# Hybrid SSD and RG-LRU block: 28 column tiles of the input projection computed in pairs of seven half-block products

## Chip, cores and metric

One core of a Trainium2 chip. The metric is the device time of one execution in microseconds (us); the kernel before takes 2112.51 us, the median of three runs (2111.7 to 2112.93).

## What is computed

One decoder block on 1024 tokens and 1024 channels, in float32:

```
hn = RMSNorm(h)
[gates | z | xBC | dt | lru_x | lru_gate] = hn @ W_in
y_ssm = W_o_ssm( GatedRMSNorm( SSD(conv(xBC)) + D*x , silu(z) ) )
y_lru = W_o_lru( RG-LRU(conv(lru_x)) * gelu(lru_gate) )
h = h + W_out( sigmoid(g_ssm) * y_ssm + sigmoid(g_lru) * y_lru )
h = h + SwiGLU(RMSNorm(h))
```

with a final RMSNorm. W_in has 16 column tiles of 128 for the gates, 10 for lru_x (LX), 10 for lru_gate (LG), and those of z, x, B and C of the SSD. The RG-LRU is, for each of 10 columns of 128 channels, a causal conv of width 4, two 128x128 gate products with sigmoids, and a scan over the tokens; its result is multiplied by gelu of the LG column.

## The kernel before

The layout is channels on partitions and tokens along the row. Every float32 operand is split into a high and a low part in TensorE's fp32r format (`split`: ACT casts the high part, L98; DVE subtracts to get the low part, L99), and every product is three matmuls, high by high, low by high and high by low (`mm3`, L168 to 177). A projection column tile is 2 token halves x 8 channel blocks x 3 = 48 matmuls of 128x512. The instructions of an engine run in the order that a scheduler gave them; each waits for semaphores of the others. All transfers are issued in order by one queue, SP.

The stages, in order: the first four gate tiles with the norm; the SSD, 64 steps (4 groups, 2 halves, 8 chunks) between whose small products 46 projection tiles are spread as fill (`fills`); the RG-LRU stage (about 760 to 1045 us), ten times LX tile, LG tile, `lru_gates` (L785 on), then two gate tiles; w_out_ssm, w_out_lru and w_out; the FFN's input product (about 1413 to 1855), and its output product.

In the RG-LRU stage `lx_done` runs the conv (ACT L491, three DVE steps L494) and splits u; `lg_done` is the gelu (L782). `lru_gates` does 12 matmuls, four tanh or exp steps on ACT, three DVE steps (L810, L808, L811), the scan (L812) and the multiply by the gelu (L813), all on DVE. POOL has nothing there. The first eight operands of w_out_ssm (`y0`) are loaded and split in this stage.

The FFN's input product is already done in pairs. For two column tiles with weights of two 512-channel halves, and two token halves, seven products of half blocks (512 channels by 512 tokens, 4 x 3 = 12 matmuls each) take the place of eight. They need sums of weights, made by POOL for each pair (`pair_sums`, L924 to L927, into buffers of their own), sums of the operands (t1 to t4), made once in w_out's second half, and combinations of the results, made by DVE from PSUM (L1030 to L1052).

Of the kernel before, what the change touches and what calls it, by code (L numbers as in the profile page):

```python
# [67 lines left out]
def hybrid_block(ctx, tc, xT, w_in, w_dt, w_os, w_ol, w_o, w_fi, w_fo, w_fl, lru_w, params, heads, out):  # L68
# [219 lines left out]
    with ExitStack() as st1:  # L288
        cst = st1.enter_context(tc.tile_pool(name="cst", bufs=1, reuse_waits="tile", side="right"))
        dt = cst.tile([P, NCH, NH], F32, name="dt")  # L290
# [468 lines left out]
        tp = ctx.enter_context(tc.tile_pool(name="tp", bufs=NTMP, reuse_waits="tile"))  # L759
        ar0 = ctx.enter_context(tc.tile_pool(name="ar0", bufs=8, reuse_waits="tile"))  # L760


        with tc.tile_pool(name="lru", bufs=1, reuse_waits="tile", side="right") as lp, tc.tile_pool(
            name="lps", bufs=2, space=PSUM
        ) as lps:
            u_, gl_ = {}, {}

            def lx_done(j):
                def done(ps):
                    u = lp.tile([P, T], F32, name="u", bufs=2)  # L770
                    conv(u, ps, [pcol("lcw", j * 4 + i) for i in range(4)], pcol("lcb", j))
                    uh = lp.tile([P, T], F32R, name="uh")
                    ul = lp.tile([P, T], F32R, name="ul")
                    split(uh, ul, u)
                    u_[j] = u, uh, ul

                return done

            def lg_done(j):
                def done(ps):  # L780
                    gl = lp.tile([P, T], F32, name="gl")
                    S.activation(gl, ps, AF.Gelu_apprx_tanh)  # L782
                    gl_[j] = gl

                return done  # L785

            def lru_gates(j):
                u, uh, ul = u_.pop(j)
                raw = lp.tile([P, 2, P], F32, name="lraw", bufs=2)
                load(raw, lru_w[:, j])  # L790
                gw = lp.tile([P, 2, P], F32R, name="lwh", bufs=2)
                gl = lp.tile([P, 2, P], F32R, name="lwl", bufs=2)
                split(gw, gl, raw)
                th = []
                for q, bname in ((0, hbr), (1, hbi)):
                    gp = lps.tile([P, T], F32, name="gp", tag="gp")
                    for c in hcol:
                        mm3(gp[:, c], lambda k: (gw[:, q, :], gl[:, q, :]), [(uh[:, c], ul[:, c])])
                    t_ = lp.tile([P, T], F32, name=f"lth{q}", bufs=2 - q)
                    S.activation(t_, gp, AF.Tanh, bias=bname[:, j : j + 1], scale=0.5)  # L800
                    th.append(t_)
                a = lp.tile([P, T], F32, name="a", bufs=2)
                S.activation(a, th[0], AF.Exp, bias=cc[:, j : j + 1], scale=cc[:, j : j + 1])

                S.activation(th[0], th[0], AF.Tanh, bias=ncc[:, j : j + 1], scale=ncc[:, j : j + 1])
                a2 = lp.tile([P, T], F32, name="a2")
                S.activation(a2, a, AF.Square)
                V.scalar_tensor_tensor(th[0], a2, 1.0, th[0], op0=ALU.add, op1=ALU.mult)  # L808
                S.activation(th[0], th[0], AF.Sqrt)
                V.scalar_tensor_tensor(u, th[1], 1.0, u, op0=ALU.add, op1=ALU.mult)  # L810
                V.scalar_tensor_tensor(u, u, 0.5, th[0], op0=ALU.mult, op1=ALU.mult)  # L811
                V.tensor_tensor_scan(a, a, u, 0.0, op0=ALU.mult, op1=ALU.add)  # L812
                V.tensor_tensor(a, a, gl_.pop(j), op=ALU.mult)  # L813
                store(yl_d[j], a)

            for j in range(NLRU):
                project_now(lx_done(j))
                project_now(lg_done(j))
                lru_gates(j)

            def gate_done(i):
                def done(ps):
                    gt = lp.tile([P, T], F32, name="gl")
                    S.activation(gt, ps, AF.Tanh, bias=hgb[:, i : i + 1], scale=0.5)
                    store(gate_d[i], gt)

                return done


            y0 = [act_pair(ar0, load_half(yn_d[i][:, hcol[0]])) for i in range(8)]  # L830
            for i in range(16 - last_gates, 16):
                project_now(gate_done(i))
# [58 lines left out]
    for d in range(KD):
        mg[1][d] = act_pair(ar1, res[d][:, 1, :])

    raws, wops = {}, {}

    def pair_load(j):
        raws[j] = []
        for q in range(2):
            raw = wpool.tile([P, KD, P], F32, name="raw", tag="raw", bufs=2)
            load(raw, w_fi[q * NFF + j])
            raws[j].append(raw)

    def pair_a1(j):  # L910
        raw = raws[j][0]
        hi = wpool.tile([P, KD, P], F32R, name="whi", tag="whi")
        lo = wpool.tile([P, KD, P], F32R, name="wlo", tag="wlo")
        split(hi, lo, raw)
        wops[j] = {"a11": (hi[:, 0:4, :], lo[:, 0:4, :]), "a12": (hi[:, 4:8, :], lo[:, 4:8, :])}
# [322 lines left out]
```

## Time and profile before

| what | value |
| --- | --- |
| median of three runs | 2112.51 us |
| the profiled execution | 2113.38 us |
| its span, first to last instruction | 2111.4 us |
| mean granted TensorE clock | 0.989 |
| TensorE, DVE, ACT, POOL busy | 98%, 60%, 41%, 19% |
| RG-LRU stage, 800 to 1000 us: TensorE, DVE, ACT | 100%, 59%, 65% |

A busy share is an average over stages; how a stage stands is read from the table of busy times by stretch, and what TensorE waited for from its list of waits. A matmul's recorded duration (about 390 ns) is longer than its distance to the next one, since matmuls are pipelined; the distance comes from how many start in a stretch.

### The profile page before, as it was taken

What the parts mean: (1) busy time and instruction counts of PE and PEld (TensorE: products, weight loads), DVE (VectorE), ACT (ScalarE), POOL (GpSimd) and SP (SyncE); (2) the same over time, 40 slices, a digit from 0 to 9 for tenths busy, and PEclk for the clock granted to TensorE, in tenths of its full rate; (3) what the DMA queues carried; (4) which work ended last, traced back from release to release, by engine and by line L of the source; (5) the groups of instructions that cost most, each with busy time, mean ns of one, the idle gap of its engine ahead of it and who ended that gap; (6) DMA issues with size and microseconds to landing.
All of it is one profiled execution on the core that took longest, in us unless ns stands there. A gap on an engine that the chain in (4) does not pass through costs nothing.

```text
span 2111.4 us, 24842 instructions
## 1 busy us (share of the span) xinstructions
PE 2066.4 (98%) x9702; PEld 1681.2 (80%) x9702; DVE 1261.3 (60%) x1587; ACT 856.0 (41%) x1253; POOL 406.7 (19%) x378
## 2 busy tenths in 40 slices
PE   8999999999999999999999999988999999999998
PEld 6677887887887888888888888866888888878887
DVE  8655567567667546555514544588666666654336
ACT  5334445445455436666513221453223222233124
POOL 5103333334343410000000000234322332100000
PEclk8999999999999999999999999999999999999999
DMA  3222223323223243211314431542222222283122
GB/s 140 88 62 88 85 77 117 103 75 113 88 77 118 89 159 135 75 65 60 128 52 159 144 114 58 162 148 97 67 87 90 82 70 88 74 287 107 52 59 80
DMA packets 99973, 212.17 MB, mean 100 GB/s; under 512 B 11024, under 2 KB 29456, under 8 KB 99856
## 3 DMA queue, kind: packets, MB, share of 16 engines
q1 hardware_dynamic: 99856, 210.59, 30.9%
q8 instruction: 76, 1.25, 0.2%
q14 instruction: 41, 0.34, 0.1%
HBM read 168.34 MB, written 42.21 MB: 100 GB/s over the span
## 4 chain that ended last, share of the span: by engine, by line
PE 87%; DVE 5%; issue 2%; POOL 2%; ACT 2%; DMA 1%; SPq 0%; DVEq 0%; POOLq 0%; ACTq 0%
PE pj L175 12%; PE pj L177 11%; PE pj L176 11%; PE pbk L175 9%; PE pbk L177 9%; PE pbk L176 9%; PE pbk L960 6%; PE pbk L962 6%; PE pbk L961 6%; PE yb L661 1%; PE yb L649 1%; DVE xs L494 1%; PE tr L627 1%; DVE wlo L99 1%; DVE xl L332 1%
## 5 line engine op out<-in xcount | busy, mean ns | idle before, releaser
L175 PE MATMUL pj<-hnh,whi 128*128 128x512 f32 x1152 | 461.0, 400 | 0.0
L177 PE MATMUL pj<-hnl,whi 128*128 128x512 f32 x1152 | 452.8, 393 | 0.0
L176 PE MATMUL pj<-hnh,wlo 128*128 128x512 f32 x1152 | 451.7, 392 | 0.0
L177 PE MATMUL pbk<-un,whi 128*128 128x512 f32 x816 | 317.8, 390 | 1.3 <-DVE un L99 1.3
L175 PE MATMUL pbk<-un,whi 128*128 128x512 f32 x816 | 317.9, 390 | 1.0 <-ACT un L98 1.0
L176 PE MATMUL pbk<-un,wlo 128*128 128x512 f32 x816 | 317.3, 389 | 0.0
L98 ACT CAST whi<-raw 128x1024 fp32r<-128x1024 f32 (+3 forms) x172 | 167.2, 972 | 308.8 <-PE pbk L177 199.7
L99 DVE TENSOR_TENSOR wlo<-raw,whi 128x1024 fp32r<-128x1024 f32 (+3 forms) x172 | 201.5, 1172 | 142.8 <-ACT whi L98 140.9
L177 PEld LDWEIGHTS pj<-hnl,whi 128*128 128x128 f32 x1152 | 216.6, 188 | 48.1 <-issue 0.5
L175 PEld LDWEIGHTS pj<-hnh,whi 128*128 128x128 f32 x1152 | 216.7, 188 | 45.8 <-issue 2.4
L176 PEld LDWEIGHTS pj<-hnh,wlo 128*128 128x128 f32 x1152 | 216.9, 188 | 44.9 <-issue 1.4
L177 PEld LDWEIGHTS pbk<-un,whi 128*128 128x128 f32 x816 | 153.2, 188 | 35.2 <-DVE un L99 3.2
L175 PEld LDWEIGHTS pbk<-un,whi 128*128 128x128 f32 x816 | 153.2, 188 | 33.3 <-ACT un L98 1.7
L176 PEld LDWEIGHTS pbk<-un,wlo 128*128 128x128 f32 x816 | 153.2, 188 | 31.8 <-issue 0.2
L960 PE MATMUL pbk<-xh,sh 128*128 128x512 f32 x352 | 140.1, 399 | 13.2 <-ACT sh L98 10.0
L857 POOL TENSOR_TENSOR rs<-rs,sq 128x512 f32<-128x512 f32 x14 | 22.7, 1620 | 639.2 <-ACT sq L856 639.2
L961 PE MATMUL pbk<-xh,sl 128*128 128x512 f32 x352 | 137.3, 390 | 0.4 <-DVE sl L99 0.4
L962 PE MATMUL pbk<-xl,sh 128*128 128x512 f32 x352 | 137.3, 390 | 0.0
L620 ACT ACTIVATE E<-csb,cs 128x128 f32<-128x128 f32 x256 | 82.8, 392 | 107.6 <-PE yb L661 100.4
L98 ACT CAST sh<-s 128x1024 fp32r<-128x1024 f32 x44 | 46.3, 1052 | 171.3 <-PE pbk L961 157.8
L960 PEld LDWEIGHTS pbk<-xh,sh 128*128 128x128 f32 x352 | 66.1, 188 | 35.1 <-ACT sh L98 10.4
L1089 DVE TENSOR_TENSOR res<-res,pbk 128x512 f32<-128x512 f32 x48 | 32.8, 686 | 87.4 <-PE pbk L177 87.4
(265 smaller groups left out, 3366.3 us busy)
## 6 DMA issues: line engine op xcount, KB each, us to landing
raw<-in_w_in SPq DMA_DIRECT2D x74, 512.0 KB, 3.5
raw<-in_w_fi SPq DMA_DIRECT2D x44, 512.0 KB, 3.9
csb<-cs_d SPq DMA_DIRECT2D x64, 256.0 KB, 3.5
ld<-act_d SPq DMA_DIRECT2D x44, 256.0 KB, 5.4
yn_d<-xs SPq DMA_DIRECT2D x16, 512.0 KB, 3.2
ld<-yn_d SPq DMA_DIRECT2D x32, 256.0 KB, 5.2
raw<-in_w_os SPq DMA_DIRECT2D x16, 512.0 KB, 3.5
gt<-gate_d SPq DMA_DIRECT2D x32, 256.0 KB, 4.1
```

Source lines behind the costliest of these rows:

```text
L98: S.copy(hi, src)
L99: V.tensor_tensor(lo, src, hi.bitcast(F32), op=ALU.subtract)
L175: PE.matmul(ps, wh, xh, start=i == 0, stop=False)
L176: PE.matmul(ps, wl, xh, start=False, stop=False)
L177: PE.matmul(ps, wh, xl, start=False, stop=i == n - 1)
L332: V.scalar_tensor_tensor(lo, x, pcol("n1", k), hi.bitcast(F32), op0=ALU.mult, op1=ALU.subtract)
L620: S.activation(E[:, j, :], csb[:, j, :], AF.Relu, bias=cs[:, c, h0 + j : h0 + j + 1], scale=-1.0)
L857: G.tensor_tensor(acc, acc, sq, op=ALU.add)
L960: PE.matmul(ps, wh, xh, start=first and k == 0, stop=False, skip_group_check=True)
L961: PE.matmul(ps, wl, xh, start=False, stop=False, skip_group_check=True)
L962: PE.matmul(ps, wh, xl, start=False, stop=last and k == 3, skip_group_check=True)
L1089: V.tensor_tensor(r, r, ps, op=ALU.add)
```

## The change

Gates 6 to 15 and LX and LG 1 to 9, 28 tiles, are taken out of the SSD's fill and the RG-LRU stage and computed as 14 pairs of seven products, in the order LX1/LG1, LX2/LG2, gates 6/7, LX3/LG3, and so on. LX0 and LG0 are still computed directly, and only gates 4 and 5 stay in the SSD's fill (38 fill tiles). In detail:

- hn is stored to memory as it is made (16 stores), reloaded behind the SSD, and made into t1 to t4 by `t_parts` (four subtractions or additions L837 to L840 and two splits for each of four channel blocks).
- `pair_sums` (L809 to L812) leaves three of its four sums in the raw weight buffers themselves; these are freed only when the last split of the pair (`pair_s`) has read them.
- The RG-LRU of a column is a generator, `lru`, with a piece run between the products of the next pair (`pump`). Its last multiply goes from DVE to POOL.
- Combinations: `c11` (ACT copies or the gate's tanh), then DVE L870, L874, L875, L879 and L883; the FFN uses the same `pair`.
- The operands of w_out_ssm are no longer loaded ahead. w_out's second half goes through columns 4 to 7 first, then 0 to 3, with `t_parts` on the latter. FFN results are stored per column instead of per half.
- Pools: room of hn's second half, blocks 0 to 3 (`hnq`), is taken over by the buffers of the pair stage (`ar` with 30 units and `sp1`).

```diff
-            fills[g, 0] = x_tiles(g, 1) + z_tiles(g, 0) + [PJ_GATE + gate_next + i for i in range(n)]
+        fills[g, 0] = x_tiles(g, 1) + z_tiles(g, 0)
...
+                    store(hn_d[k][:, hcol[h]], xr[h][k])
...
+    def pair_sums(n):
+        g_, u_ = raws[n]
+        s1 = sp1.tile([P, H], F32, name="ws1", tag="ws1")
+        wops[n]["raw1"] = s1
+        G.tensor_tensor(blk(s1), u_[:, 0:4, :], u_[:, 4:8, :], op=ALU.add)
+        G.tensor_tensor(u_[:, 0:4, :], u_[:, 0:4, :], g_[:, 0:4, :], op=ALU.add)
+        G.tensor_tensor(g_[:, 0:4, :], g_[:, 0:4, :], blk(s1), op=ALU.add)
+        G.tensor_tensor(g_[:, 4:8, :], g_[:, 4:8, :], g_[:, 0:4, :], op=ALU.add)
...
+    def pair(n, x, c11, pump, nxt=None, first=False, cpool=None):
+        wo = wops.pop(n)
...
+        px, pv = bank(), bank()
+        product(px, wo["a11"], x["b11"], True, False)
+        S.copy(c1[:, 0, :], px)
+        pump()
...
+            product(pv, wo["s1"], x["t1"], True, False)
+            pump()
+            product(px, wo["a12"], x["b21"], False, True)
+        prep(pair_a1)
+        prep(pair_sums)
+        py = bank()
+        product(py, wo["s2"], x["t2"], True, False)
+        c11(c0, px)
+        V.tensor_tensor(c0[:, 1, :], c1[:, 0, :], py, op=ALU.subtract)
+        pump()
+        product(py, wo["s3"], x["t3"], False, True)
+        prep(pair_s1)
+        V.tensor_tensor(c1[:, 0, :], py, c1[:, 0, :], op=ALU.subtract)
+        V.tensor_tensor(c1[:, 1, :], c1[:, 0, :], pv, op=ALU.subtract)
+        pump()
+        pz = bank()
+        product(pz, wo["a22"], x["t4"], True, True)
+        V.tensor_tensor(c1[:, 0, :], pz, c1[:, 0, :], op=ALU.add)
+        prep(pair_s, 1)
+        pump()
+        product(pv, wo["s4"], x["b22"], False, True)
+        V.tensor_tensor(c0[:, 1, :], c0[:, 1, :], pv, op=ALU.add)
+        prep(pair_s, 0)
+        pump()
+        return c0, c1
...
+    for k in range(4):
+        t_parts(x1, k, bs.pop(k), bs.pop(k + 4))
...
+    for n, (f0, f1) in enumerate(ppairs):
+        nxt = n + 1 if n + 1 < len(ppairs) else None
+        if nxt:
+            pair_load(nxt, [w_in[f] for f in ppairs[nxt]])
+        if f0 >= PJ_LX:
+            c0, c1 = pair(n, x1, copy_c11, pump, nxt)
+            sides.append(lru(f0 - PJ_LX, c1, c0))
...
-    res = [unit(ar1, F32, "res") for d in range(KD)]
+    yn = [load_acts(yn_d[:8], h) for h in range(2)]
```

How the order moves on DVE, at three places. First the entry into the RG-LRU stage. Before, behind the SSD's last reciprocals: splits of weights (wlo, lwl), the last scaling of the SSD's results (xs) and the conv of LX0 (u, L494):

```order
L99 TENSOR_TENSOR wlo<-raw,whi 128x1024
L713 SCALAR_TENSOR_TENSOR xs<-xs,par,acc 128x1024 x4
L99 TENSOR_TENSOR wlo<-raw,whi 128x1024
L99 TENSOR_TENSOR lwl<-lraw,lwh 128x256
L494 SCALAR_TENSOR_TENSOR u<-pj,par,u 128x1023
L99 TENSOR_TENSOR wlo<-raw,whi 128x1024
L494 SCALAR_TENSOR_TENSOR u<-pj,par,u 128x1022
L99 TENSOR_TENSOR lwl<-lraw,lwh 128x256
L494 SCALAR_TENSOR_TENSOR u<-pj,par,u 128x1021
```

And with the change; b is reloaded hn, xth and xtl are the split t operands:

```order
L838 TENSOR_TENSOR b<-b 128x512
L99 TENSOR_TENSOR lw<-lraw,lw 128x256
L839 TENSOR_TENSOR b<-b 128x512
L840 TENSOR_TENSOR b<-b 128x512
L99 TENSOR_TENSOR xtl<-b,xth 128x1024
L837 TENSOR_TENSOR b<-b 128x512
L99 TENSOR_TENSOR xtl<-b,xth 128x1024
L838 TENSOR_TENSOR b<-b 128x512
L839 TENSOR_TENSOR b<-b 128x512
L840 TENSOR_TENSOR b<-b 128x512
L505 SCALAR_TENSOR_TENSOR u<-pj,par,u 128x1023
L99 TENSOR_TENSOR xtl<-b,xth 128x1024
```

The conv of LX0 now stands behind three groups of t operands; its other two steps follow with the third group's last split between them.

Second, inside the stage with the change, pair 2 (gates 6 and 7) with the RG-LRU of columns 1 and 2 beside it; pbk is a PSUM bank, c_ the two result tiles of a pair, the rows on a, u and lth are the RG-LRU's:

```order
L924 SCALAR_TENSOR_TENSOR u<-u,lth_6646 128x1024
L870 TENSOR_TENSOR c_6713<-c_6714,pbk 128x512
L925 SCALAR_TENSOR_TENSOR a<-a,u 128x1024
L505 SCALAR_TENSOR_TENSOR u<-c_6544,par,u 128x1023
L99 TENSOR_TENSOR lw<-lraw,lw 128x256
L505 SCALAR_TENSOR_TENSOR u<-c_6544,par,u 128x1022
L874 TENSOR_TENSOR c_6714<-pbk,c_6714 128x512
L505 SCALAR_TENSOR_TENSOR u<-c_6544,par,u 128x1021
L875 TENSOR_TENSOR c_6714<-c_6714,pbk 128x512
L879 TENSOR_TENSOR c_6714<-pbk,c_6714 128x512
L99 TENSOR_TENSOR ul<-u,uh 128x1024
L99 TENSOR_TENSOR wsl<-raw,wsh 128x1024
```

Between the first and the second reading of a product's bank (L870, L874) stand the scan and two conv steps.

Third, the exit. Before, in the end of the RG-LRU stage; un are the split operands of w_out_ssm's second half of tokens, those of the first half were made earlier:

```order
L811 SCALAR_TENSOR_TENSOR u<-u,lth_8163 128x1024
L99 TENSOR_TENSOR wlo<-raw,whi 128x1024
L812 SCALAR_TENSOR_TENSOR a<-a,u 128x1024
L813 TENSOR_TENSOR a<-a,gl 128x1024
L99 TENSOR_TENSOR wlo<-raw,whi 128x1024
L99 TENSOR_TENSOR un<-ld,un 128x512 x8
L99 TENSOR_TENSOR wlo<-raw,whi 128x1024 x7
```

With the change:

```order
L879 TENSOR_TENSOR c_8417<-pbk,c_8417 128x512
L919 SCALAR_TENSOR_TENSOR u<-lth_8512,u 128x1024
L921 SCALAR_TENSOR_TENSOR lth_8487<-a_8538,lth_8487 128x1024
L883 TENSOR_TENSOR c_8416<-c_8416,pbk 128x512
L924 SCALAR_TENSOR_TENSOR u<-u,lth_8487 128x1024
L925 SCALAR_TENSOR_TENSOR a<-a,u 128x1024
L99 TENSOR_TENSOR un<-ld,un 128x512 x16
L99 TENSOR_TENSOR wlo<-raw,whi 128x1024 x7
```

All 16 splits of w_out_ssm's first operands stand behind the last scan.

## Rows read from the trace of the kernel before

**Rows 1.** The page, busy time, share of the span and count by engine.

```profile
PE 2066.4 (98%) x9702; PEld 1681.2 (80%) x9702; DVE 1261.3 (60%) x1587; ACT 856.0 (41%) x1253; POOL 406.7 (19%) x378
```

**Rows 2.** Table by stretch: PE, PEld, DVE, ACT, POOL busy (count), clock, DMA share, GB/s.

```profile
760.00:800.00 40.00, 40.00 (x174) 32.49 (x173) 25.52 (x24) 20.61 (x26) 0.00 (x0) 1.00 0.66 231
800.00:900.00 100.00, 100.00 (x438) 81.91 (x437) 59.30 (x49) 65.73 (x62) 0.00 (x0) 1.00 0.25 84
...
1400.00:1500.00 100.00, 85.24 (x362) 67.67 (x361) 81.58 (x84) 40.48 (x56) 41.75 (x28) 0.95 0.29 96
1500.00:1600.00 100.00, 100.00 (x438) 81.20 (x437) 67.01 (x78) 28.20 (x36) 29.49 (x21) 1.00 0.26 80
...
1440.00:1850.00 410.00, 406.77 (x1776) 330.62 (x1776) 273.47 (x317) 116.41 (x150) 117.50 (x82) 1.00 0.27 84
160.00:750.00 590.00, 586.41 (x3120) 473.71 (x3117) 384.07 (x540) 281.82 (x503) 205.41 (x233) 1.00 0.30 93
```

**Rows 3.** TensorE's waits: waiting line, releaser, us in all, times, longest.

```profile
PE pbk L960 <- ACT sh L98: 10.0, 1, 10.0
...
PE st L177 <- POOL xddl L638: 3.2, 8, 1.1
```

**Rows 4.** Table by stretch around the start of the FFN.

```profile
1420.00:1424.00 4.00, 0.00 (x0) 0.00 (x0) 3.87 (x5) 0.70 (x2) 1.52 (x1) 0.65 0.00 0
1424.00:1428.00 4.00, 0.00 (x0) 0.00 (x0) 3.43 (x3) 2.14 (x4) 3.93 (x3) 0.50 0.17 66
1428.00:1432.00 4.00, 3.43 (x6) 1.63 (x7) 4.00 (x4) 3.81 (x7) 2.36 (x2) 0.57 0.16 32
1432.00:1436.00 4.00, 4.00 (x20) 3.24 (x19) 4.00 (x6) 1.64 (x2) 0.00 (x0) 1.00 0.49 168
```

**Rows 5.** Groups of DVE instructions in the RG-LRU stage: busy us, mean ns | idle before.

```profile
L99 DVE TENSOR_TENSOR wlo<-raw,whi 128x1024 fp32r<-128x1024 f32 x21 | 25.6, 1221 | 23.9 <-ACT whi L98 23.9
L812 DVE TENSOR_TENSOR_SCAN a<-a,u 128x1024 f32<-128x1024 f32 x10 | 22.8, 2281 | 0.0
L494 DVE SCALAR_TENSOR_TENSOR u<-pj,par,u 128x1023 f32<-128x1023 f32 x10 | 12.8, 1280 | 13.8 <-ACT u L491 13.8
...
L810 DVE SCALAR_TENSOR_TENSOR u<-lth,u 128x1024 f32<-128x1024 f32 x10 | 12.2, 1225 | 38.5 <-ACT lth L800 38.5
...
L99 DVE TENSOR_TENSOR un<-ld,un 128x512 fp32r<-128x512 f32 x8 | 5.0, 684 | 0.0
L99 DVE TENSOR_TENSOR lwl<-lraw,lwh 128x256 fp32r<-128x256 f32 x10 | 4.2, 420 | 8.4 <-ACT lwh L98 8.4
```

**Rows 6.** Groups of DVE instructions in the FFN pairs, 1440 to 1850.

```profile
L1044 DVE TENSOR_TENSOR sg<-sg,s 128x512 f32<-128x512 f32 x21 | 34.0, 1618 | 0.7
...
L1043 DVE TENSOR_TENSOR s<-s,rs 128x512 f32<-128x512 f32 x21 | 22.7, 1082 | 0.7
...
L1033 DVE TENSOR_TENSOR u<-s,pbk 128x512 f32<-128x512 f32 x22 | 15.1, 688 | 9.1 <-PE pbk L962 9.1
```

**Rows 7.** Groups of POOL instructions in the FFN pairs, 1440 to 1850.

```profile
L927 POOL TENSOR_TENSOR s<-s,raw 128x512 f32<-128x512 f32 x21 | 35.9, 1711 | 0.2
L926 POOL TENSOR_TENSOR s<-raw 128x512 f32<-128x512 f32 x20 | 29.1, 1456 | 15.0 <-PE pbk L962 15.0
L925 POOL TENSOR_TENSOR s<-s,raw 128x512 f32<-128x512 f32 x21 | 27.6, 1317 | 1.5
L924 POOL TENSOR_TENSOR s<-raw 128x512 f32<-128x512 f32 x20 | 25.8, 1288 | 243.1 <-DVE sl L99 236.2 <-DVE su L1038 6.9
```

**Rows 8.** The page's DMA issues, KB each, us from issue to landing.

```profile
raw<-in_w_in SPq DMA_DIRECT2D x74, 512.0 KB, 3.5
```

**Rows 9.** Groups of ACT instructions in the RG-LRU stage, 780 to 1045.

```profile
L98 ACT CAST whi<-raw 128x1024 fp32r<-128x1024 f32 x22 | 22.8, 1036 | 1.9 <-PE pj L177 1.9
...
L782 ACT ACT_TABLE_LOAD x10 | 12.8, 1283 | 0.2
...
L782 ACT ACTIVATE gl<-pj 128x1024 f32<-128x1024 f32 x10 | 10.3, 1028 | 2.6 <-PE pj L177 2.6
```

More of the change, by code (lines that the diff above doesn't have):

```diff
@@ L61 @@
 NTMP = 13
-NUNIT = 29
+NUNIT = 30
 FFG = ((0, 6), (6, 12), (12, 17), (17, 22))
@@ L757, in hybrid_block @@
                 pass
[L759 to L832, printed above, removed]
@@ new lines, in hybrid_block, with hn_load, lx0_done @@
+    x1 = {
+        "b11": [hn[0][k] for k in range(4)],
+        "b21": [hn[0][4 + k] for k in range(4)],
+        "b22": [hn[1][4 + k] for k in range(4)],
+        **{t: [None] * 4 for t in ("t1", "t2", "t3", "t4")},
+    }
+    bs = {}
+    def hn_load(k):
+        for i in (k, k + 4):
+            bs[i] = unit(ar, F32, "b")
+            load(row(bs[i]), hn_d[i])
+    u0, gl0 = unit(ar, F32, "u"), unit(ar, F32, "c1")
+    def lx0_done(ps):
+        conv(row(u0), ps, [pcol("lcw", i) for i in range(4)], pcol("lcb", 0))
@@ new lines, in lg0_done @@
+    def lg0_done(ps):
+        S.activation(row(gl0), ps, AF.Gelu_apprx_tanh)
+    hn_load(0)
+    hn_load(1)
+    pieces = [project(lx0_done), project(lg0_done)]
+    for k in range(4):
+        t_parts(x1, k, bs.pop(k), bs.pop(k + 4))
+        if k < 2:
+            hn_load(k + 2)
+        if k == 3:
+            pair_load(0, [w_in[f] for f in ppairs[0]])
+        for _ in range(2):
+            next(pieces[k // 2], None)
+    for q in pieces:
+        for _ in q:
+            pass
+    pair_a1(0)
@@ L848, in mm_act, with load_acts @@
+    while sides:
+        pump()
+    st_hn.close()
+    st_br = ExitStack()
+    br = st_br.enter_context(tc.tile_pool(name="br", bufs=6, reuse_waits="tile", side="right"))
+    st_tp = ExitStack()
+    tp = st_tp.enter_context(tc.tile_pool(name="tp", bufs=11, reuse_waits="tile", side="right"))
+    def load_acts(srcs, h, pool=None):
+        return [act_pair(pool or ar, load_half(s[:, hcol[h]])) for s in srcs]
     def mm_act(ps, w, xs):
@@ L889, in hybrid_block @@
             V.tensor_tensor(r, r, gt, op=ALU.add)
-        mg[0][d] = act_pair(ar0, res[d][:, 0, :])
+        mg[0][d] = act_pair(ar, res[d][:, 0, :])
     for d in range(KD):
[L892 to L915, printed above, removed]
@@ L956, in product @@
-    def product(ps, w, x, first, last):
-        for k in range(4):
-            wh, wl = w[0][:, k, :], w[1][:, k, :]
-            xh, xl = (t_[:, k % 2, :] for t_ in xop[x][k // 2])
-            PE.matmul(ps, wh, xh, start=first and k == 0, stop=False, skip_group_check=True)
-            PE.matmul(ps, wl, xh, start=False, stop=False, skip_group_check=True)
-            PE.matmul(ps, wh, xl, start=False, stop=last and k == 3, skip_group_check=True)
-    rs2 = [keep.tile([P, H], F32, name=f"rs2{h}") for h in range(2)]
@@ L1070, in last_w @@
             load(raw, w_fl[i])
-            wl.append(act_pair(pool, raw))
+            wl.append(act_pair(ar, raw))
     def load_group(gi):
         k0, k1 = FFG[gi]
-        return [load_acts(ar0 if gi == len(FFG) - 1 and h else ar2, act_d[k0:k1], h) for h in range(2)]
+        return [load_acts(act_d[k0:k1], h) for h in range(2)]
     acts = [None] * len(FFG)
```

324 lines of the change are left out of this document (194 added, 130 removed).

## Prediction

> **What bounds the kernel now.** I read the page's busy shares first: TensorE has work for 98% of the span, DVE for 60%, POOL for 19% [rows 1]. TensorE's time is the kernel's time as long as nothing makes it wait, so the second view is the table by stage. In the RG-LRU stage (800 to 1000) TensorE is busy all the time with 438 matmuls in 100 us, so one 128x512 matmul costs 100/438 = 0.228 us [rows 2]; the reader should see that DVE is at 59% there and POOL at nothing. The FFN pairs (1500 to 1600) have the same 438. The SSD stretch (160 to 750) is busy for 586.41 of 590 us. Third are TensorE's waits: they are small, and the one long one is 10.0 us at the first product of the first FFN pair [rows 3]. The table of 4 us steps shows what comes with it: no matmul from 1420 to 1428, granted clock 0.65 and 0.50, six matmuls in the next 4 us at 0.57, then 20 [rows 4]. So a stall before a stage costs its length and about 2 us more. What the change is worth hangs on one question: does TensorE stay as full in the new stage, whose operands are made by DVE, ACT and POOL while it runs?
>
> **A. Matmuls removed.** 14 pairs take 7 x 12 = 84 matmuls where two tiles took 96: 168 fewer, 168 x 0.228 = **-38.3 us** [rows 2]. Everything else is what this exposes.
>
> **B. The SSD with 38 fill tiles for 46.** Eight tiles x 48 x 0.228 = 87.5 us of matmuls leave a stage in which they were cover; DVE's 384 us there shrink only by eight splits of 1.22 us [rows 2, 5], so its share goes from 65% to about 74%. A step of the last half group keeps 24 fill matmuls (5.5 us) against 205/64 = 3.2 us of POOL work [rows 2]. Bounds: 0, and 8 us if each of that half group's eight steps loses 1; the 3.2 us of POOL waits of now [rows 3] are nearest. **+3.**
>
> **C. Entry into the pair stage.** The first order excerpt is the place. The second reload of hn and POOL's first sum use room of hn tiles that the 32nd matmul of LG0 reads last, 32 x 0.228 = 7.3 us after LG0 starts; with 3.5 us for 512 KB [rows 8] the operand is there at 10.8, while LG0 ends at 48 x 0.228 = 10.9. From there DVE has, in its order, three operand groups of 4 x 0.69 + 2 x 1.22 = 5.2 us (all but one subtraction), a 0.42 us split and the conv's three steps of 1.28 [rows 5, 6]: 15.6 - 0.7 + 0.4 + 3.8 = 19.1. The first product takes LX0's PSUM and waits for the last conv step, at 29.9: idle 19.0. POOL's four sums beside it stretch some DVE steps (L1044 takes 1.62 where L1033, with one operand in PSUM, takes 0.69 [rows 6]): +2. In pair 0 the copy of the first product stands on ACT behind two casts, a table load, the gelu and two casts (4 x 1.04 + 1.28 + 1.03 [rows 9]) and comes about 4 us after 24 matmuls are through; the slow restart is hidden in it. Together **+25**. Bounds: 10, the stall of [rows 3], and 32.
>
> **D. Inside the pair stage.** A pair is 19.15 us of TensorE, and 21.9 with the 12 RG-LRU matmuls. DVE needs 1.22 + 0.69 + 2 x 1.22 for the splits and 5 x 0.69 for the combinations, 7.8 us; an RG-LRU column three conv steps 3.8, split 1.22, weight split 0.42, three of 1.225 and the scan 2.28, 11.4 [rows 5, 6]. 19.2 of 21.9: it fits, but DVE works in order, and a product that adds onto a bank waits until DVE has read it. The second excerpt is pair 2 (gates 6 and 7). From the end of its s2 product: L870 0.69, only then may s3 run (until 3.5); DVE goes on with scan 2.28, conv 1.28, weight split 0.42, conv 1.28 (5.9), L874 0.69, conv 1.28, L875 0.69 (8.6), for which s4 waits, while TensorE is through s3 and the 5 matmuls left at 4.7. Lost: 0.8 + 3.9 = 4.7 us. The same count over pairs 1 to 7 gives 3.0, 4.7, 2.5, 0, 3.5, 2.1 and 0; the last three, repeated, add 11: 27 in all. Against it stands that the FFN's pairs, with the same read-before-add, lose 410.00 - 406.77 = 3.2 us over 21 pairs [rows 2]. Bounds 4 and 33; nearer to the count, since the FFN has no scan and conv in DVE's queue: **+20**.
>
> **E. Exit to w_out_ssm.** Before, the first half's operands were loaded and split during the stage (8 x 0.684 [rows 5]) and nothing waited. Now (third excerpt) all 16 stand behind the last scan. From the last matmul: ACT has two table loads, tanh and sqrt left, the scan ends at about 5, operand 0 is split at 5.7, then one per 0.69 us; the load of operand 5 waits on SP behind the store of the last RG-LRU column, which waits for POOL's multiply (about 2 x 1.29, an estimate from the 512 wide sum [rows 7]). Eleven loads of 256 KB at the 231 GB/s of [rows 2] take 12 us more, so the first 48 matmuls (10.9 us) end at about 24. **+12**; bounds 4 (the scan alone) and 15.
>
> **F. FFN start.** Before, the window 1400 to 1500 holds 362 matmuls for 438: 76 x 0.228 = 17 us lost [rows 2]. Now w_out's second half runs columns 4 to 7 first, so t parts come one column at a time: 5.2 us plus the column's own 0.69 + 1.22 of DVE against 5.5 of TensorE. DVE ends some 5 to 8 us behind. **-9**, bounds -15 and -2.
>
> **G. The rest.** FFN pairs keep 84 matmuls, and a raw pair that is freed later (load 3.5 [rows 8], cast 1.04 and subtraction 1.22 [rows 5, 9], sums 5.8 [rows 7]) still fits into 19. FFN-out's first operands now wait for the FFN's pools to close, and the 16 stores of hn stand on SP ahead of early loads: **+2**, bounds 0 and 7. The yl store, res copy on ACT and merged act stores are hidden by TensorE work; without that cover they cost under 1 us each.
>
> **Sum.** -38.3 + 3 + 25 + 20 + 12 - 9 + 2 = +14.7. The profiled execution took 2113.4, 0.9 above the median of the runs shown, 2112.5; on the median **2127 us**.
>
> **Rivals.** *TensorE stays fed* (faster). The stage as a whole has room: DVE 14 x 7.8 + 10 x 11.4 = 223 of 295 us. If the orders' waits are mostly met in time, D is 5 and E 5, B is 0, G 0, F -12, and C its bare 19 us: -38.3 + 29 - 12 = -21, **2091**. For it: the FFN pairs' 3.2 us. Against: C is fixed by the order and the pair counted above has no second cover. It decides for faster where C, D and E cost under 38 together (57 in the forecast).
> *POOL's sums make DVE the bound* (slower still). Four sums are 1.29 + 1.46 + 1.32 + 1.71 = 5.8 us a pair [rows 7]; if all of it lengthens DVE, an RG-LRU pair needs 25.0 against 21.9: 3.1 x 9 = 28, with 5 of waits D is 33, **2140**. For: L1044's 1.62. Against: in an FFN pair POOL's 5.8 us cost DVE 1.6 to 1.8 us (L1044 and L1043 over 0.69 [rows 6], and little else). It decides from 2.7 us a pair on. The Trainium skill, "SBUF — State Buffer", section "Who interferes with whom", states that a DVE instruction with two SBUF inputs and a reading GpSimd instruction exclude each other, the later one fully blocked; by that rule this rival would be the forecast. The rows bear it out in part: L1044 loses 0.9 of a possible 1.3 to 1.7.
> *The SSD misses its cover*: each of the 64 steps loses 0.2 us, B is 13, **2137**; POOL's 205 us there are against it [rows 2].
>
> **How the numbers follow.** Forecast 0.45, fed 0.30, DVE bound 0.15, SSD 0.10. A measurement of this kernel can tell about 0.2%, 4.2 us, from no change: under 2108.3 is faster, over 2116.7 slower. Faster 0.29 (the fed case, nearly whole), same 0.10 (tails of the forecast and of the fed case), slower 0.61. The forecast's own range by its bounds is 2110 to 2142. The whole runs from **2088** (the fed case's middle, with 3 us) to **2146** (DVE bound and 6 us), with a tenth left out on either side.
>
> **What would show it.** After: an idle stretch of 15 to 25 us on TensorE before the first pair product, with the conv's last step (L505) as releaser and a low granted clock behind it; waits for L870, L875 and L883's chain of 1 to 5 us in most pairs; a gap of 8 to 14 us before the first w_out_ssm matmuls, released by un splits; at the FFN start under 8 us. Wrong would be: pair stage at 100% busy (fed), DVE over 95% there (DVE bound), or idle TensorE in SSD steps.

## Result and profile after

The changed kernel takes 2197.55 us (median of four runs, 2196.53 to 2200.0) against 2112.11 for the kernel before beside it: a ratio of 1.0408, 95% interval 1.039 to 1.0426. It is 85 us slower; forecast were 15, and the range ended at 2146. The sign was right, the size was not.

The page's busy line of the changed kernel answers to [rows 1]:

```profile
PE 2074.4 (95%) x9534; PEld 1666.3 (76%) x9534; DVE 1356.9 (62%) x1651; ACT 894.1 (41%) x1308; POOL 532.9 (24%) x440
```

168 matmuls are gone, as counted, yet TensorE is busy longer and for less of the span. The table by stretch, with the columns of [rows 2], shows where (first line: the SSD; the pair stage runs from 739.5 to 1116):

```profile
160.00:670.00 510.00, 500.22 (x2711) 399.37 (x2710) 365.92 (x523) 259.20 (x479) 207.61 (x229) 1.00 0.30 92
700.00:800.00 100.00, 71.37 (x270) 55.99 (x269) 62.76 (x59) 45.19 (x51) 22.90 (x13) 0.81 0.23 84
800.00:900.00 100.00, 88.83 (x350) 69.54 (x349) 69.80 (x58) 58.70 (x66) 37.16 (x19) 0.91 0.21 73
900.00:1000.00 100.00, 88.15 (x362) 69.07 (x360) 72.30 (x59) 59.88 (x69) 35.28 (x18) 0.97 0.23 78
1000.00:1100.00 100.00, 87.02 (x357) 68.61 (x357) 72.38 (x61) 52.22 (x60) 32.57 (x15) 0.97 0.22 77
```

Where 438 matmuls ran in 100 us before, 350 to 362 run now. Busy is only 11 to 13 points down, the count 17 to 20%: matmuls also take longer, and the granted clock says why. DVE is at 70 to 72%, far from full. TensorE's waits, with the columns of [rows 3]:

```profile
PE pbk L830 <- DVE c L870: 25.0, 9, 3.6
PE pbk L830 <- DVE u L505: 20.7, 1, 20.7
PE pbk L179 <- ACT un L98: 10.8, 4, 5.8
PE pbk L186 <- POOL rs L1033: 8.4, 1, 8.4
PE pbk L179 <- ACT uh L98: 6.7, 5, 2.9
PE pbk L830 <- DVE c L875: 6.1, 2, 5.7
PE st L179 <- ACT xddh L648: 5.9, 8, 1.7
```

L505 is the entry (term C), un the exit (E; 4.7 of its 10.8 us come later, at the FFN's output product), rs the FFN's start (F), xddh the SSD (B). L870 and L875 are the combinations that must read a bank before the next product adds onto it, uh the RG-LRU's operand: these are D. The groups of DVE in the pair stage (740 to 1110; busy us, mean ns of one) answer to [rows 5]:

```profile
L99 DVE TENSOR_TENSOR wsl<-raw,wsh 128x1024 fp32r<-128x1024 f32 x28 | 38.7, 1386 | 7.6 <-ACT wsh L98 7.6
L925 DVE TENSOR_TENSOR_SCAN a<-a,u 128x1024 f32<-128x1024 f32 x9 | 24.3, 2704 | 0.1
L99 DVE TENSOR_TENSOR wlo<-raw,whi 128x1024 fp32r<-128x1024 f32 x15 | 22.4, 1493 | 11.4 <-ACT whi L98 11.4
L99 DVE TENSOR_TENSOR ws1l<-ws,ws1h 128x512 fp32r<-128x512 f32 x13 | 19.2, 1479 | 7.1 <-ACT ws1h L98 7.1
L505 DVE SCALAR_TENSOR_TENSOR u<-c,par,u 128x1021 f32<-128x1021 f32 x9 | 18.5, 2057 | 0.2
...
L99 DVE TENSOR_TENSOR lw<-lraw,lw 128x256 fp32r<-128x256 f32 x9 | 12.4, 1373 | 0.0
...
L874 DVE TENSOR_TENSOR c<-pbk,c 128x512 f32<-128x512 f32 x14 | 9.6, 686 | 21.4 <-PE pbk L832 21.4
```

The scan is at 2.70 us for 2.28, the last conv step at 2.06 for 1.28 (the two before it at 1.81 and 1.46), a split of 256 columns at 1.37 for 0.42. L874, with one operand in PSUM, has its 0.69. On POOL, in the same stretch, the sums that took 1.3 to 1.7 in the FFN before [rows 7], and the RG-LRU's multiply:

```profile
L926 POOL TENSOR_TENSOR a<-a,c 128x1024 f32<-128x1024 f32 x9 | 28.7, 3187 | 15.8 <-DVE a L925 15.8
L809 POOL TENSOR_TENSOR ws<-raw 128x512 f32<-128x512 f32 x13 | 25.9, 1994 | 220.8 <-DMA raw<-in_w_in 220.8
```

One of the nine L870 waits in DVE's timeline (start, us):

```profile
919.96 3.37 DVE L925 TENSOR_TENSOR_SCAN a<-a,u 128x1024 f32<-128x1024 f32 x1
923.25 1.19 DVE L99 TENSOR_TENSOR wsl<-raw,wsh 128x1024 fp32r<-128x1024 f32 x1
924.37 0.67 DVE L870 TENSOR_TENSOR c<-c,pbk 128x512 f32<-128x512 f32 x1
```

and in TensorE's:

```profile
921.08 0.39 PE L830 MATMUL pbk<-xth,wsh 128*128 128x512 f32 x1
925.10 0.50 PE L830 MATMUL pbk<-xth,wsh 128*128 128x512 f32 x1 [3.63 <-DVE c L870]
...
926.32 0.63 PE L831 MATMUL pbk<-xth,wsl 128*128 128x512 f32 x1
926.75 0.63 PE L832 MATMUL pbk<-xtl,wsh 128*128 128x512 f32 x1
...
930.01 0.39 PE L830 MATMUL pbk<-xth,wsh 128*128 128x512 f32 x1
930.23 0.39 PE L831 MATMUL pbk<-xth,wsl 128*128 128x512 f32 x1
```

L870's bank is complete when the s2 product ends, at about 921.5. L870 stands behind a stretched scan and a split; TensorE idles 3.63 us. The next three matmuls start 0.33 to 0.23 us apart, then they are 0.43 us apart (926.32 to 926.75), not 0.22 (930.01 to 930.23). The table by stretch shows the granted clock at 0.61 of the full level in these 4 us, and 11 matmuls where 17 to 18 fit (4 / 0.228):

```profile
921.00:925.00 4.00, 0.47 (x3) 0.04 (x1) 4.00 (x4) 1.35 (x2) 1.71 (x2) 1.00 0.00 0
925.00:929.00 4.00, 3.90 (x11) 3.12 (x12) 3.09 (x3) 0.00 (x0) 1.67 (x1) 0.61 0.39 131
929.00:933.00 4.00, 4.00 (x18) 3.22 (x17) 2.21 (x4) 1.20 (x2) 0.00 (x0) 0.96 0.78 262
```

For some 3 us TensorE is at the lower of its two levels, 1.2 GHz.

**The ledger.** From the timelines, the stages of the two kernels and the terms of the prediction:

| term | forecast | measured | how read |
| --- | --- | --- | --- |
| A matmuls | -38.3 | -38.3 | 9702 - 9534 = 168, x 0.228 |
| B SSD | +3 | +12 | first to last SSD step 591.6 before, 518.7 after: 72.9 saved for the 372 matmuls that left this stretch, 84.8; the other 12 of the 384 left from behind the last step |
| C entry | +25 | +20.7 | idle from LG0's end (718.8) to 739.5 |
| D pair stage | +20 | +73 | 739.5 to 1116.2 is 376.6 us for 1296 x 0.228 = 295.5; of the 81 lost, waits are 49.5 (5.8 of them are E's) and matmuls at the low clock 29.5 |
| E exit | +12 | +13 | un waits: 5.8, and 7.1 more up to the FFN |
| F FFN start | -9 | -6.5 | the FFN's stage is 0.9 shorter with the 5.6 of G in it |
| G rest | +2 | +7 | 21 FFN pairs of 19.50 for 19.23, 5.6; FFN-out 4.0; start -2.3 |
| sum | +14.7 | +81 | spans: 2194.8 - 2111.4 = 83.4 |

Some 2 us of small gaps in the pair stage are in no row. 53 of the 66 us between forecast and ledger are in D.

### The profile page after: what moved, and what is told of

Read it like the earlier page. It is cut to its first block, busy times and chain, and to the rows that moved or that the text cites. A ratio compares the mean times of both kernels' runs of the same rounds, so it can differ in the third digit from the quotient of the medians.

```text
span 2194.8 us, 24745 instructions
## 1 busy us (share of the span) xinstructions
PE 2074.4 (95%) x9534; PEld 1666.3 (76%) x9534; DVE 1356.9 (62%) x1651; ACT 894.1 (41%) x1308; POOL 532.9 (24%) x440
## 4 chain that ended last, share of the span: by engine, by line
PE 75%; DVE 10%; ACT 6%; issue 4%; DMA 2%; POOL 2%; SPq 0%; DVEq 0%; POOLq 0%; ACTq 0%
PE pbk L181 9%; PE pbk L179 9%; PE pbk L180 9%; PE pbk L830 8%; PE pbk L832 8%; PE pbk L831 8%; PE pj L181 7%; PE pj L179 7%; PE pj L180 6%; DVE u L505 1%; PE yb L672 1%; PE yb L660 1%; PE tr L638 1%; DMA raw<-in_w_in 1%; DVE wlo L99 1%
## 5 line engine op out<-in xcount | busy, mean ns | idle before, releaser
L179 PE MATMUL pbk<-un,whi 128*128 128x512 f32 x816 | 320.4, 393 | 10.8 <-ACT un L98 10.8
L179 PE MATMUL pj<-hnh,whi 128*128 128x512 f32 x704 | 284.6, 404 | 0.0
L181 PE MATMUL pj<-hnl,whi 128*128 128x512 f32 x704 | 278.4, 396 | 0.0
L180 PE MATMUL pj<-hnh,wlo 128*128 128x512 f32 x704 | 276.0, 392 | 0.0
L830 PE MATMUL pbk<-xth,wsh 128*128 128x512 f32 x432 | 176.3, 415 | 25.1 <-DVE c L870 25.0
L809 POOL TENSOR_TENSOR ws<-raw 128x512 f32<-128x512 f32 x36 | 57.3, 1591 | 538.7 <-DMA raw<-in_w_fi 271.1
L831 PE MATMUL pbk<-xth,wsl 128*128 128x512 f32 x432 | 176.3, 408 | 0.0
L832 PE MATMUL pbk<-xtl,wsh 128*128 128x512 f32 x432 | 175.5, 407 | 0.0
L181 PEld LDWEIGHTS pj<-hnl,whi 128*128 128x128 f32 x704 | 132.3, 188 | 29.2 <-issue 0.7
L179 PEld LDWEIGHTS pj<-hnh,whi 128*128 128x128 f32 x704 | 132.5, 188 | 27.1 <-issue 2.6
L180 PEld LDWEIGHTS pj<-hnh,wlo 128*128 128x128 f32 x704 | 132.5, 188 | 27.0 <-issue 1.2
L830 PEld LDWEIGHTS pbk<-xth,wsh 128*128 128x128 f32 x432 | 84.3, 195 | 53.5 <-DVE c L870 35.0
```

What stands on the lines that cost most here:

```text
L179: PE.matmul(ps, wh, xh, start=i == 0, stop=False)
L180: PE.matmul(ps, wl, xh, start=False, stop=False)
L181: PE.matmul(ps, wh, xl, start=False, stop=i == n - 1)
L809: G.tensor_tensor(blk(s1), u_[:, 0:4, :], u_[:, 4:8, :], op=ALU.add)
L830: PE.matmul(ps, wh, xh, start=first and k == 0, stop=False, skip_group_check=True)
L831: PE.matmul(ps, wl, xh, start=False, stop=False, skip_group_check=True)
```

## Experiments

Each is an edit of the changed kernel, run once with a profile beside the kernel before (2110.2 to 2111.9 in all of them). The question is D. Three accounts stand against each other, and where expectations number them it is in this order: (1) **contention**: POOL's sums and DVE's steps stretch each other; (2) **the loop**: a raw buffer is free only after load, sums and split, so weights come late; (3) **order**: the RG-LRU's steps stand ahead of the combinations in DVE's queue, and short stalls bring the low clock. "Stage" is from the first pair product to the first w_out_ssm matmul, with its listed waits and its loss at the low clock.

### Leaving out the sums, or moving them

```diff
     def pair_sums(n):
...
+        if not ffn[0]:
+            wops[n]["raw1"] = u_[:, 0:4, :].rearrange("p k c -> p (k c)")
+            return
```

> Leaves out the four weight sums of the 14 pairs behind the SSD (the splits read the raw weights); the FFN keeps its sums. The pair stage now takes 377 us from its first product to the first w_out_ssm matmul, where its matmuls alone would need 296: 50 us of waits and 30 us at the low clock. Theory 1 (POOL's sums and DVE's two-operand steps stretch each other, and the stretched scan, conv and splits hold up the combinations): time falls by about 50 us, to 2147, and the scan, conv and split rows return to 2.28, 1.28 and 1.22 us but for the multiply on POOL. Theory 2 (in-place sums close a loop of load, sums and splits that is longer than a pair): also about 50 us less, but with stretched rows only where the multiply runs. Theory 3 (only DVE's order, RG-LRU steps ahead of the combinations): 10 us less at most, 2187.

2165.31, halfway between the accounts: stage 346.7, waits 33.8, low clock 15.7. On DVE the scan is back at its own time, but what meets the multiply (L930 here) on POOL is not:

```profile
L929 DVE TENSOR_TENSOR_SCAN a<-a,u 128x1024 f32<-128x1024 f32 x10 | 22.9, 2287 | 0.2
...
L505 DVE SCALAR_TENSOR_TENSOR u<-c,par,u 128x1022 f32<-128x1022 f32 x9 | 17.6, 1958 | 0.1
```

One of these meetings, first in DVE's timeline, then in POOL's:

```profile
804.73 1.26 DVE L505 SCALAR_TENSOR_TENSOR u<-c,par,u 128x1023 f32<-128x1023 f32 x1
805.90 2.60 DVE L99 TENSOR_TENSOR lw<-lraw,lw 128x256 fp32r<-128x256 f32 x1
808.42 1.27 DVE L505 SCALAR_TENSOR_TENSOR u<-c,par,u 128x1022 f32<-128x1022 f32 x1
```

```profile
805.04 3.18 POOL L930 TENSOR_TENSOR a<-a,c 128x1024 f32<-128x1024 f32 x1 [26.73 <-DVE a L929]
```

The conv step that ran when the multiply came keeps its 1.26. The split of 0.42 us that came during the multiply takes 2.60 and ends 0.3 us after it (808.22). In each of the ten multiplies of e1 a DVE step with two SBUF operands that starts during it is 1.5 to 2.2 us longer than alone: the step that comes second waits for the first.

The sums cost 32 us, 30 of them in the stage; 49.5 of the stage's 81 us of loss stay without them.

```diff
+        E = G if ffn[0] else V
-        G.tensor_tensor(blk(s1), u_[:, 0:4, :], u_[:, 4:8, :], op=ALU.add)
+        E.tensor_tensor(blk(s1), u_[:, 0:4, :], u_[:, 4:8, :], op=ALU.add)
...
```

> The same four sums of these 14 pairs by DVE instead of POOL; nothing left out. DVE gets 4 x 0.69 = 2.8 us more per pair, 21.9 of the 21.9 us that TensorE needs in a pair with RG-LRU. Theory 1: the stretch goes, 35 us less, about 2160. Theory 2: the sums get shorter (2.8 for 5 to 11 us), so the loop is shorter too: 25 us less, 2172. Theory 3: more work in the queue that is late already, 10 us or more longer, 2207.

2185.46. The sums take 1.18 + 3 x 0.69 = 3.2 us a pair on DVE, and still the kernel is 12 us faster than with them on POOL: POOL's "free" work cost more than DVE doing it. Not the 25 or more expected: waits stay at 50.3 (longer queue), the low clock falls to 19.1.

```diff
-    ar = st_ar.enter_context(tc.tile_pool(name="ar", bufs=NUNIT, reuse_waits="tile"))
+    ar = st_ar.enter_context(tc.tile_pool(name="ar", bufs=NUNIT - 1, reuse_waits="tile"))
...
+            for i in range(4):
+                G.tensor_tensor(junk, hn[0][i][0].bitcast(F32), hn[0][i + 4][0].bitcast(F32), op=ALU.add)
+            return
```

> POOL makes four sums of the same size per pair behind the SSD, but of parts of hn and into a tile that nobody reads; the splits take the raw weights as they are, so no split and no load waits for a sum (the pool of units is one shorter for the tile). The sums of the weights are left out. Theory 1: as slow as the change, 2197 within 12 us, with stretched DVE rows. Theory 2: 50 us less, as with no sums at all. Theory 3: 10 us less at most.

2201.07, in all as slow as the change. But 14 us of it are at the entry (34.6 for 20.7; 18.0 in e1), where these sums, which wait for no load, run beside the t operands. In the stage, sums of the same size that nothing waits for cost 19 of the 30 us that the real ones cost: 366.0, against 346.7 in e1 and 376.6 in the change. Groups of DVE; without any sums, in e1, the three have 1.39, 2.29 and 1.28:

```profile
L99 DVE TENSOR_TENSOR wsl<-raw,wsh 128x1024 fp32r<-128x1024 f32 x28 | 42.7, 1526 | 27.3 <-ACT wsh L98 27.3
L932 DVE TENSOR_TENSOR_SCAN a<-a,u 128x1024 f32<-128x1024 f32 x9 | 21.6, 2397 | 0.2
...
L505 DVE SCALAR_TENSOR_TENSOR u<-c,par,u 128x1021 f32<-128x1021 f32 x8 | 11.2, 1404 | 0.1
```

So in the stage about two thirds of what the sums cost is their running beside DVE. The other 10.6 us are left for the loop, or for what else differs here (one buffer fewer, other moments for the sums); no run separates these.

### Leaving out the RG-LRU

```diff
-    sides = [lru(0, gl0, u=u0)]
+    sides = []
+    store(yl_d[0], row(gl0))
...
-            sides.append(lru(f0 - PJ_LX, c1, c0))
+            store(yl_d[f0 - PJ_LX], row(c1))
```

> Leaves out the RG-LRU of all ten columns in the pair stage (the conv of columns 1 to 9, splits, gate products, activations, scan, multiply); the projections stay. 120 matmuls, 27 us, go with it. Theory 3: nearly all waits and low clock go too, 27 + 70 less, about 2100. Theory 1: nothing is left in the queue that a sum could stretch but the splits: 27 + 60 less, 2110. Theory 2: the loop of load, sums, split stays, shorter by the stretch alone: 27 + 30 less, 2140.

2127.03, 70.5 less; 27.4 of that are the RG-LRU's own 120 matmuls. The stage still waits for 26.2 and loses 10.7 at the low clock, now for L875 (13.3 in seven) and L870 (7.7, once, in the first pair). DVE is busy for only 36 to 39% (800 to 1000 us). One wait for L875 in the timelines of POOL, ACT, DVE and TensorE:

```profile
894.40 1.38 POOL L809 TENSOR_TENSOR ws<-raw 128x512 f32<-128x512 f32 x1 [12.98 <-DMA raw<-in_w_in]
895.81 0.62 ACT L98 CAST ws1h<-ws 128x512 fp32r<-128x512 f32 x1 [2.45 <-POOL ws L809]
896.46 1.23 DVE L99 TENSOR_TENSOR ws1l<-ws,ws1h 128x512 fp32r<-128x512 f32 x1 [1.25 <-ACT ws1h L98]
897.61 0.67 DVE L875 TENSOR_TENSOR c<-c,pbk 128x512 f32<-128x512 f32 x1
898.34 0.51 PE L830 MATMUL pbk<-hnh,wsh 128*128 128x512 f32 x1 [1.71 <-DVE c L875]
```

The first sum waits for its load, ACT and DVE wait for the sum, and L875 stands behind that split in DVE's queue. This is the second account, weights that come late, and it needs no RG-LRU.

> Leaves out both the RG-LRU and the four weight sums in the pair stage. Without the RG-LRU alone the time was 2127.0, with 26 us of waits and 11 us at the low clock left in the stage. If those are POOL's sums (stretch or late weights), they go too: 2105 or less. If they are the pair itself (a product that waits until DVE has read its bank, with little else for TensorE to do), they stay: 2120 or more.

Both edits together: 2103.57, 23.5 less than with the sums, and the waits for L875 are gone (0.2 left). TensorE is full, as this table shows (columns of [rows 2]); waits are 8.4:

```profile
800.00:900.00 100.00, 99.82 (x430) 79.77 (x429) 38.45 (x47) 29.03 (x36) 0.00 (x0) 1.00 0.26 93
900.00:1000.00 100.00, 99.90 (x431) 79.84 (x430) 38.73 (x48) 27.04 (x34) 0.00 (x0) 1.00 0.26 94
```

So pairs without sums, loads and splits included, keep TensorE busy. Of e1's 2165.31, 61.7 go with the RG-LRU: 27.4 of matmuls and 34 of stalls.

### The multiply, alone and with the sums

```diff
-        G.tensor_tensor(a, a, row(gl), op=ALU.mult)
+        V.tensor_tensor(a, a, row(gl), op=ALU.mult)
```

> Only the RG-LRU's last multiply goes back from POOL to DVE, where the kernel before has it: DVE gets 10 x 1.21 us, POOL loses 10 x 3.3. If POOL's stretch of DVE is what costs (the sums elsewhere cost as much as the sums themselves), the 33 us of POOL taken out pay more than the 12 us of DVE put in: 5 to 10 us faster, about 2190. If DVE's queue length alone counts, 5 to 12 us slower.

2193.26, 3.3 us under the fastest of the four runs of the change: the direction that contention gives, in one run and less than the 5 to 10 expected. Splits of s weights are back at 1.22, and DVE's queue is 1.22 us longer per column (L870 waits 44.7 in ten).

> The four sums left out in the pair stage and the multiply on DVE: POOL has nothing to do there. With the sums left out alone the time was 2165.3, with 33.8 us of waits and 15.7 at the low clock in the stage. What is left then can only be DVE's order and its own length: if the rest was still the multiply's stretch, 8 us less or more, 2157; if it is order, 2160 to 2172, with the waits for the combinations where they are.

e1 and e9 together, no POOL work in the stage: 2161.22, stage 343.1, waits 29.5, low clock 16.7. Groups of DVE, then the two largest waits:

```profile
L99 DVE TENSOR_TENSOR wsl<-raw,wsh 128x1024 fp32r<-128x1024 f32 x28 | 34.1, 1219 | 16.6 <-ACT wsh L98 16.6
L929 DVE TENSOR_TENSOR_SCAN a<-a,u 128x1024 f32<-128x1024 f32 x10 | 22.9, 2287 | 0.2
...
L505 DVE SCALAR_TENSOR_TENSOR u<-c,par,u 128x1021 f32<-128x1021 f32 x9 | 11.5, 1277 | 0.1
```

```profile
PE pbk L834 <- DVE c L874: 19.2, 9, 4.0
PE pbk L834 <- DVE u L505: 18.1, 1, 18.1
```

Every DVE step has the duration of [rows 5], and TensorE still waits 19.2 for L874 (L870 of the changed kernel). The prediction's count by order is 27; the waits here are 29.5 - 5.8 = 23.7 without the exit's. In e1 they are 28.0, but 11.2 of that are for the RG-LRU's operands uh and ul, which the count does not have.

### The clock

```diff
+        pz = bank()
+        if not first and x is not x_ffn[0]:
+            for i in range(8):
+                PE.matmul(pz, wo["s2"][0][:, i % 4, :], x["t2"][i % 4][0], start=i == 0, stop=i == 7, skip_group_check=True)
         product(py, wo["s3"], x["t3"], False, True)
...
-        pz = bank()
```

> Eight more matmuls in each of the 14 pairs, ahead of the s3 product, into the bank that the a22 product overwrites afterwards: 112 x 0.228 = 25.5 us of work that no result uses, at the place where TensorE waits longest for DVE (25.0 us for L870 in nine waits). If the low clock behind these waits is a cost of its own (30 us in the stage), the matmuls take the place of the wait, the clock stays up there, and the kernel with more work is 8 to 15 us faster, about 2186. If the clock has nothing to do with the idle time, or the matmuls come too early, it is 5 to 25 us slower, 2203 to 2223.

A miss: 2209.6. The 112 matmuls (25.5 us) halve the L870 waits (12.6 for 25.0), but others grow (uh 13.3 for 6.7), and the low clock still costs 21.6 for 29.5. The low clock does fall by 8 us, but the added matmuls cost more: here cover put at one wait moved most of the stall to the next.

### Entry, SSD, tail

```diff
+    for _ in pieces[0]:
+        pass
     for k in range(4):
         t_parts(x1, k, bs.pop(k), bs.pop(k + 4))
...
-        for _ in range(2):
-            next(pieces[k // 2], None)
+        next(pieces[1], None)
```

> LX0's pieces are issued ahead of the t operands, so the conv's steps stand behind three quarters of one group on DVE and no more behind three. If the idle stretch ahead of the first pair product (20.7 us) is set by the conv's place alone, it falls to about 8 us and the kernel is 12 us faster. If the 20.8 us of t operands behind the late reload are the limit, the wait only moves from the first product to the s1 product, and the gain is 5 us or less.

2196.84: the conv ahead of the t operands cuts the entry's wait from 20.7 to 9.4, and the stage grows from 376.6 to 385.7, since the t operands are now late (9.9 us of new waits for them and for the first copy). DVE's total at the entry decides, not who is first.

```diff
-        fills[g, 0] = x_tiles(g, 1) + z_tiles(g, 0)
+        fills[g, 0] = x_tiles(g, 1) + z_tiles(g, 0) + [PJ_GATE + gate_next + i for i in range(n)]
...
-        if j % 2 == 0:
-            ppairs.append(gpairs.pop(0))
```

> Gates 6 to 13 stay in the SSD's fill, as in the kernel before, and only 10 pairs are left (LX and LG 1 to 9, gates 14 and 15). 4 x 12 = 48 matmuls come back, 11.0 us. The SSD loses its 14.6 us no more (72.9 us shorter in the change where eight tiles are 87.5). If gate pairs only cost, 4 x 5 us of stage losses go too: 2175. If they give DVE the time to catch up with the RG-LRU, the nine columns in a row lose more: 2195 or above.

Gates 6 to 13 back in the SSD's fill, ten pairs left: 2211.29, 14 us slower than the change. The SSD takes 592.0 us again, the 591.6 of before, so B is what the eight tiles covered (the expectation's 14.6 counts all 384 matmuls of the eight tiles, but 372 of them left the SSD's stretch: 11.9). But the ten pairs, 960 matmuls in 313.6 us, lose 63.4 in waits and 30.0 at the low clock; the largest wait is

```profile
PE pbk L180 <- ACT uh L98: 30.3, 6, 11.9
```

Gate pairs carry no column of their own: as the expectation's second case has it, they were what gave DVE time for the RG-LRU.

```diff
-    for k in range(4):
-        t_parts(x1, k, bs.pop(k), bs.pop(k + 4))
...
+    for j in range(NLRU):
+        order += [PJ_LX + j, PJ_LG + j]
```

> The SSD with its 46 tiles, the RG-LRU stage and the operands of w_out_ssm loaded ahead as in the kernel before; from w_out_ssm on as in the change (order of w_out's second half, sums in place, shared pair, merged stores). The change gained 6.5 us at the FFN's start, and lost 5.6 in its pairs (19.50 for 19.23 us each) and 4.0 in its output product. If these are all, 2114 within 5 us; the whole loss of the change is then ahead of w_out_ssm.

The SSD, RG-LRU stage and early loads of the kernel before, with only the FFN and FFN-out of the change: 2119.25, 9 over the kernel before, at the upper edge of what was expected. From the first w_out_ssm matmul on it is 7.3 us longer (10.3 in the change). The rest of the 85 us lies ahead of that point.

```diff
-                pair_sums(0)
-                pair_s1(0)
...
+    pair_sums(0)
+    pair_s1(0)
```

> At the FFN's start the four sums of the first pair are issued behind the last column's sum of squares, not ahead. In the change TensorE waits 8.4 us there for the last sum of squares (L1033); DVE's steps beside the sums took 1.75 for 0.69 us. If the sums' place is the cause, 5 us less, 2192; if the queue of t operands on DVE is (5.2 us and 1.9 per column for 5.5), the wait moves to the s2 product and nothing changes within 2 us.

2201.06, and it decides nothing: POOL's order came out as it was, and the rs wait is 8.4 as before the edit. Whether POOL's first sums delay the FFN's start stays open.

## Why the prediction was wrong

**The step that failed is D**: 20 forecast, 73 measured. It has three parts, and the count of the first was right. With POOL quiet (e12), 23.7 us of waits and 16.7 at the low clock are left, 40 of the 73; POOL's work makes the other 33.

*The order.* The count of 27 at durations without contention holds: 23.7 with POOL quiet. It holds by place too. For pairs 1 to 7 it was 3.0, 4.7, 2.5, 0, 3.5, 2.1 and 0; TensorE's waits for the combinations there are 2.6, 5.8, 2.2, 0, 2.6, 3.6 and 0 in the change, and 4.0, 2.3, 0.7, 0, 4.0, 0.9 and 0 in e12. What the count left out are the waits for the RG-LRU's own operands, uh and ul: 12.4 of the 43.7 in the change, none in e12. The error was to shade it to 20 because the FFN's pairs lose only 3.2: "the FFN has no scan and conv in DVE's queue" was the reason against, and it was the one that counted. No run put the combinations ahead of the scan, so that a reordering would win these back is not shown; leaving out the RG-LRU does (e5 against e1).

*The contention.* The text priced it at "little else" in the FFN and gave D none of it. e1 and e12 put POOL's share at 32 to 36 us of the kernel's time with its clock loss, 30 to 33 of the stage's. Of the sums' 30, e3 shows 19 as contention; the rest stays open between late weights, which e4 shows at work without the RG-LRU, and e3's other differences. The prediction had no late weights in D: it looked at a raw pair that is freed later only for the FFN's pairs (G). The FFN was the wrong place to read contention from: there a stretched step delays nobody for long. In the pair stage the stretched conv and scan stand ahead of the combinations.

*The clock.* [rows 4] were read as "about 2 us more" for a 10 us stall and used in C, but short stalls in D pay too. Matmuls at the low level cost 29.5 us in the change against 43.7 of waits, and 16.7 with POOL quiet; some 2.6 of the 29.5 follow the entry's stall. They do not pay alike: behind waits of 1.45 to 1.59 us the matmuls lost 0.3 us each, behind most of 1.8 to 5.8 us between 1.7 and 3.5, and behind one of 3.56 us, at 1081, only 0.4, with the granted clock at 1.00. D's upper bound of 33 counted waits alone.

**B** was mis-sized, 3 against 12 and a bound of 8. The rival "the SSD misses its cover" had its size, 13, and e7 shows that the eight tiles were that cover; that each step loses 0.2 us is not shown. Idle time explains half: the listed waits are 9.7 us (4.5 before), and TensorE is busy for 500.22 of 510 us against 586.41 of 590 [rows 2]. The other 6 us are inside what counts as busy, as longer distances between the SSD's small matmuls; what they come from stays open. Judging from listed waits ([rows 3], 3.2) was the error; only the length of the stretch against the count of its matmuls shows the whole.

**A, C, E and F** came out near their sizes. C's idle at the entry is 20.7 for 19 counted with 2 on top; the 4 for the copy on ACT are not there (a wait of 0.2), and the slow restart is in D's clock loss. E's chain is as told but for its first link: the first operand waits 5.8 us for ACT's cast, which stands behind two table loads, and not for the scan. Then come the splits behind the scan, and loads behind the store that waits for POOL's multiply (2.63 us for 2 x 1.29). But its 13 for 12 is in part luck: 7.6 are waits, and the granted clock is near 0.5 from 1116 to 1124, which the sum did not have. The FFN's start waits 8.4 for 10.0, not under 8 as foretold, and its releaser is now the last sum of squares on POOL, not the t operands. **G** is 7 for 2: each FFN pair lost 0.27 us, 0.11 of it in the product behind L870, the rest in some 5 ns more per matmul whose cause stays open.

**The rivals.** "TensorE stays fed" is refuted: 87 to 89% busy. "POOL's sums make DVE the bound" named the right cause and the wrong mechanism: DVE stays at 70 to 72% in the full stage, and what hurts is not its sum of work but when the combinations come. The Trainium skill, "SBUF — State Buffer", section "Who interferes with whom", states that a DVE instruction with two SBUF inputs contends with a GpSimd instruction that reads SBUF, and one with at most one SBUF input, outside the two-port modes, does not. The trace agrees on both: 2.06 for 1.28 on a conv step that now reads SBUF, 0.69 unchanged on L874. The rows of e1 also bear out the prediction's words "the later one fully blocked": a split of 0.42 us took 2.60. The prediction used the rule only to ask whether DVE would fill up.

No variant that computes the whole result beats the kernel before. Even without POOL's work the change is at 2161, and e5's 2103.57 lacks 27.4 us of matmuls that the result needs.

## What to carry to other kernels

Where products add onto a bank that another engine has to read first, walk that engine's queue in order, with the durations that its steps have beside their neighbours, and take the count as it comes out; a busy share of 72% says nothing about when. Count TensorE's stalls with the matmuls at the low clock behind them: in the runs with the RG-LRU those added between four and seven tenths of the waits (19.1 to 44.5 us in e2, 16.7 to 23.7 in e12). Work given to POOL is free only where DVE's steps of two SBUF operands have slack and no split that DVE's queue needs early waits for it: here the sums cost 32 us, and 20 on DVE itself. Projection tiles that serve as fill are worth less than their matmuls when taken out, here 72.9 of 84.8 us.

## What the runs showed of the hardware

Both sides of the contention stretch over a stage, though in a single meeting it is the one that comes second (e1's rows): POOL's sums took 1.7 to 2.0 us in the pair stage for 1.3 to 1.7 in the FFN before, its multiply 3.2, while the scan went from 2.28 to as much as 3.37 and a split of 256 columns from 0.42 to 1.37. That a stall as short as 3.6 us brought about 3 us of matmuls at 0.43 apart was not expected from the one long stall of [rows 4].
